# A hybrid decoder trunk on one core: gate weights loaded among the first values, more partners at the phase's front, a pair's copies in one turn, the last root ahead of the last products

## The chip, the cores and the metric

The kernel runs on one core of a Trainium2 chip. The time is the device time of one execution in microseconds (us); the median of the runs shown is what is compared. A profile is one more execution, recorded by the hardware profiler. Its engines are PE (TensorE, the matmuls; PEld is its loading of the stationary operand), DVE (VectorE), ACT (ScalarE), POOL (GpSimd) and SP (SyncE, which here only issues transfers). A name with a q behind it (SPq, POOLq) is the instruction queue of that engine. "L444" is line 444 of the kernel.

## The reference

One decoder layer over 256 tokens of width 2048, all in 32-bit floats:

```python
h = rmsnorm(x, pre_norm_g)
a_q, a_k, a_v, a_g, a_lr, b_q, b_k, b_v, b_g, m_a, m_b = split(h @ w_in)

gk  = log_sigmoid(a_lr @ gla_gk_w2 + gla_gk_b) / 16          # forget gate, rank 16
o_a = gla_chunked(a_q, a_k, a_v, gk)                         # 4 heads, gated linear attention
y_a = (rmsnorm(o_a, gla_norm_g) * silu(a_g)) @ w_branch_a

o_b = diff_attention(b_q, b_k, b_v, lam)                     # 16 heads, softmax1 - lam * softmax2
y_b = (rmsnorm(o_b, diff_norm_g) * (1 - lam_init) * silu(b_g)) @ w_branch_b

out = (sigmoid(m_a) * y_a + sigmoid(m_b) * y_b) @ w_out
x   = x + rmsnorm(out, post_norm_g)
```

The weights take 201 MB and are read once from memory; most of the work is the matmuls of 256 tokens with these weights.

## The kernel before

**Halves.** Every weight matrix is read in tiles of up to 1 MB ("raw", three buffers) and used in two halves. `seq` lists all halves in the order of their use. For each half, `emit_half` splits the 32-bit weights into two parts: ACT rounds to the matmul's format (L261, "hi"), DVE subtracts that from the original (L262, "lo"). TensorE then multiplies hi with both parts of the tokens and lo with the first part. The hi and lo buffers are three each, and `take` lets the splits be written three halves ahead of the matmuls (AHEAD = 3). So the split of a half can run once TensorE has done with the half three before it. The tile of a half is loaded by SP, two halves ahead in the list (`load`), once one of the three raw buffers is free.

**The order of each engine.** Instructions are written in program order, and a planner then fixes the order of each engine's queue ahead of time, by when it reckons that an instruction's inputs are there and by the program order among those that are ready. `tc.keep_in_program_order(i)` puts i behind the instruction that was written just before it on the same engine; `tc.issue_after(i)` puts the TensorE instructions of a block behind i. Once built, each engine works through its queue in order.

**Side tasks.** Work beside the large products is written as generators in the list `tasks`; each `pump` advances the first one or two of them by one step (a "turn"). A task that has yielded "go" is also advanced by `pump_eager`, which stands in the middle between two pumps.

**Stages.** In the order of the program:

1. `first_joint` multiplies the first values (v0, 16 halves of 832 columns). From kt = 11 on each half pumps `load_constants` once: constants, three loads of masks. Then come v2 and v3 (`token_major`, 8 halves each), with pumps of two tasks after each half: `late`, `forget_gate` and `sum_operands`.
2. `forget_gate` zeroes a tile (L515), loads w2 into four strips of it (L517, POOL), waits a turn, transposes the low-rank columns, splits w2 (L533 to L535), and multiplies (L544).
3. The phase (L779 to L788). Six sets of weight columns are multiplied with seven products in place of eight (PRODUCTS = 1, 3, 5, 6, 2, 7, 4), two tiles each, which makes 6 x 7 x 2 = 84 slots of two halves. A product needs sums of weight blocks. Blocks a and b are loaded by `link`, c by SP; further blocks are added to a and b in place by POOL's accumulating transfers (L198) and by DVE (L206). After product 1 has split a tile of a, the transfer that adds to it is issued; product 5 uses the result. Each slot is followed by one half of other work ("partner"): v4, k and q, the first two groups' dq and dk, and m00, 80 halves in all. Four slots, (s, 2, 0) for s = 1 to 4, have no partner, so that the counts agree. Within the phase every matmul is pinned to the program order.
4. Gated linear attention (`gla_scores`, `gla_out`), then differential attention in pairs of heads (`diff_pair`), beside the products of the gates and branches. A pair loads its q into kh and its k into kl (`twice`), copies kh to q2 (L960, ACT), subtracts into q2 from kh (L963, DVE), yields "go", copies kl over kh (L965, ACT) and subtracts (L966, DVE). The scores' matmuls (L982, L983) follow a pump later.
5. The output products for column groups 0 to 2 go over both token blocks; group 3 is kept split in memory and multiplied first for block 0 (512 columns), then for block 1 in two banks of 256 columns. Each bank's squares go to ACT with a running sum (L1150), its product with the norm's gain to DVE (L1154). The root of a block is a power on POOL (L352). The block is then scaled and added to x in four parts (L1170), each of which is stored by SP or ACT as `PARTS` says (L1171).

Of the kernel before, what the change touches and what calls it, by code (L numbers as in the profile page):

```python
# [8 lines left out]
BF16 = mybir.dt.bfloat16  # L9
U8 = mybir.dt.uint8  # L10
AF = mybir.ActivationFunctionType
ALU = mybir.AluOpType
AX = mybir.AxisListType

P = 128
D = 2048
# [6 lines left out]
RANK = 16  # L23
# [4 lines left out]
PRODUCTS = (1, 3, 5, 6, 2, 7, 4)  # L28
SETS = 6
# [5 lines left out]
PARTS = ((0, 768, 0), (1024, 1664, 1), (1664, 2048, 0), (768, 1024, 1))  # L35
# [40 lines left out]
def phase_steps():  # L76

    keys = ["v4"] + [f"{name}{hf}{c}" for hf in range(2) for name in ("k", "q") for c in range(4)]
    keys += [f"{name}{g}{c}" for g in EARLY for pair in range(2) for name in ("dq", "dk") for c in (2 * pair, 2 * pair + 1)]
    keys += ["m00"]  # L80
    other = [(key, r, h) for key in keys for r in range(4 if key in ("v4", "m00") else 1) for h in range(2)]
    slots = [(s, prod, t) for s in range(SETS) for prod in PRODUCTS for t in range(2)]
    skip = [(s, 2, 0) for s in range(1, SETS)][: len(slots) - len(other)]
    mixed = []
    for slot in slots:
        mixed += [("set", *slot, h) for h in range(2)]
        if slot not in skip:
            mixed.append(other.pop(0))
    return mixed + other

# [2 lines left out]
def hybrid_kernel(ctx: ExitStack, tc, xt, xn, preg, postg, w, w2, gkb, glag, lamv, diffg, ident_d, causal_d, lmask_d, out):  # L93
    nc = tc.nc
    pe, act, dve, pool, sp = nc.tensor, nc.scalar, nc.vector, nc.gpsimd, nc.sync
# [12 lines left out]
    def u(shape, name, dtype=F32):  # L108
        count[0] += 1
        return big.tile(shape, dtype, tag="u", name=f"{name}_{count[0]}")  # L110
# [5 lines left out]
    def sm(shape, name, dtype=F32, bufs=2):  # L116
        count[0] += 1
        return pools[0].tile(shape, dtype, tag=name, name=f"{name}_{count[0]}", bufs=bufs)
# [197 lines left out]
    diffg_s = const.tile([P, 1], F32, name="diffg_s")  # L316
    lam_s = sm([P, 4, 64], "lam_s", bufs=1)

    def load_constants():
        tc.keep_in_program_order(sp.dma_start(ident, ident_d))  # L320
        for t, src in ((gkb_s, gkb), (glag_s, glag), (diffg_s, diffg), (causal, causal_d)):
            tc.keep_in_program_order(sp.dma_start(t, src))
        tc.keep_in_program_order(sp.dma_start(lam_s, lamv.partition_broadcast(P)))
        yield
        for n in range(0, len(LEVELS) + 2, 4):
            m = min(4, len(LEVELS) + 2 - n)
            t = u([P, 4, S], "lmask")
            tc.keep_in_program_order(sp.dma_start(t[:, :m, :], lmask_d[:, n : n + m, :]))
            pool.tensor_copy(lmask[:, n : n + m, :], t[:, :m, :])
            yield  # L330

    ones = const.tile([P, P], F32, name="ones")
    dve.memset(ones, 1.0)
# [174 lines left out]
    def lend(tag, name, dtype=F32):  # L508

        count[0] += 1  # L510
        return blocks.tile([P, 8, P], dtype, tag=tag, name=f"{name}_{count[0]}", bufs=1).rearrange("p a t -> p (a t)")

    def forget_gate():
        w2_raw = lend("s2h", "w2_raw")
        tc.keep_in_program_order(dve.memset(w2_raw, 0.0))  # L515
        for i in range(4):
            pool.dma_start(w2_raw[32 * i : 32 * i + RANK, :], w2)  # L517
        yield
        yield
        bank = ps("bg")  # L520
        for b in range(2):
            pe.transpose(bank[:, P * b : P * b + P], lr[:, b, :], ident)
        top = t2([P, 512], "lrh").bitcast(F32R)
        lrt = sm([P, S], "lrt", F32R, bufs=1)
        act.activation(top[:, :S], bank[:, :S], AF.Copy)
        for i in (0, 64):
            act.activation(lrt[i : i + 32, :], bank[i : i + 32, :S], AF.Copy)
            r = slice(i + 32, i + 64)
            dve.tensor_tensor(out=lrt[r, :], in0=bank[r, :S], in1=f32(top[r, :S]), op=ALU.subtract)
        w2_s = lend("s2l", "w2_s", F32R)  # L530
        top = lend("r3h", "w2h", F32R)
        r = slice(64, P)
        act.activation(w2_s[:64, :], w2_raw[:64, :], AF.Copy)  # L533
        act.activation(top[r, :], w2_raw[r, :], AF.Copy)
        dve.tensor_tensor(out=w2_s[r, :], in0=w2_raw[r, :], in1=f32(top[r, :]), op=ALU.subtract)  # L535
        yield
        gp.extend(u([P, 2, 4, P], "gp") for _ in range(2))
        for hf in range(2):
            for c in range(2):
                bank = ps("bg")  # L540
                for i in range(2):
                    ct = 4 * hf + 2 * c + i
                    o = bank[:, S * i : S * i + S]
                    pe.matmul(o, w2_s[:, P * ct : P * ct + P], lrt, start=True, stop=True)  # L544
                for i in range(2):
                    ct = 4 * hf + 2 * c + i
                    act.activation(gp[hf][:, :, 2 * c + i, :], bank[:, S * i : S * i + S].rearrange("p (b t) -> p b t", b=2), AF.Identity, bias=gkb_s[:, ct : ct + 1])
            yield
        e = [lend(tag, "e") for tag in ("r3h", "r3l")]
        z = [t.rearrange("p b c t -> p (b c t)") for t in gp]  # L550
        for hf in range(2):
            act.activation(e[hf], z[hf], AF.Abs)
            yield
            act.activation(e[hf], e[hf], AF.Exp, scale=-1.0)
            yield
        for hf in range(2):
            act.activation(e[hf], e[hf], AF.Ln, bias=1.0)
        for hf in range(2):
            yield
            dve.scalar_tensor_tensor(out=z[hf], in0=z[hf], scalar=0.0, in1=e[hf], op0=ALU.min, op1=ALU.subtract)  # L560
        done.add("gate")
# [368 lines left out]
    for g in range(4):  # L930
        banks = token_major(f"ag{g}", 512, x_ops, 2)
        t = u2([P, 2, 512], "ua")
# [15 lines left out]
    def diff_pair(g, pair, values):  # L948
# [12 lines left out]
        for m in range(2):  # L961
            other = slice(64 - 64 * m, P - 64 * m)
            dve.tensor_tensor(out=q2[other, m], in0=f32(kh[other, m]), in1=f32(q2[other, m]), op=ALU.subtract)  # L963
        yield "go"
        tc.keep_in_program_order(act.activation(kh, f32(kl), AF.Copy))  # L965
        dve.tensor_tensor(out=kl, in0=f32(kl), in1=f32(kh), op=ALU.subtract)  # L966
        yield
# [69 lines left out]
        bank = ps("bg")  # L1037
# [4 lines left out]
        lo = ol[:, 2 * pair : 2 * pair + 2, :].rearrange("p h t -> p (h t)")  # L1042
# [78 lines left out]
    for g in range(4):  # L1121
        banks = token_major(f"y1{g}", 512, b_ops, 1 if g else 2, None if g else settle)
        for b in range(2):
            t = gb[g][:, b, :]
# [11 lines left out]
    for b in range(2):  # L1136
        xres.append([])
        for i in range(2):
            t = u([P, 1024], "xres")
# [3 lines left out]
    ssq = sm([P, 2, 5], "ossq", bufs=1)  # L1143
# [4 lines left out]
    def square(b, bank, n, i):  # L1148
        junk = sm([P, 512], "junk", BF16, bufs=1)
        act.activation(junk[:, :n], bank, AF.Square, accum_out=ssq[:, b, i : i + 1])  # L1150

    def gain(b, bank, lo, n):
        c = slice(lo % 1024, lo % 1024 + n)
        return dve.tensor_tensor(out=yg[b][lo // 1024][:, c], in0=bank, in1=pg[lo // 1024][:, c], op=ALU.mult)  # L1154

    def subtotal(b, parts):
        r = sm([P, 1], "or", bufs=2)
        dve.tensor_reduce(out=r, in_=ssq[:, b, :parts], op=ALU.add, axis=AX.X)
        dve.tensor_scalar(out=r, in0=r, scalar1=1.0 / D, scalar2=EPS, op0=ALU.mult, op1=ALU.add)
        return r  # L1160

    def last_part(b, bank, lo, n, i, r):
        square(b, bank, n, i)
        tc.keep_in_program_order(gain(b, bank, lo, n))
        tc.keep_in_program_order(dve.scalar_tensor_tensor(out=r, in0=ssq[:, b, i : i + 1], scalar=1.0 / D, in1=r, op0=ALU.mult, op1=ALU.add))
        rsqrt(r, r)
        for lo, up, queue in PARTS:
            c = slice(lo % 1024, lo % 1024 + up - lo)
            t, x = yg[b][lo // 1024][:, c], xres[b][lo // 1024][:, c]
            tc.keep_in_program_order(dve.scalar_tensor_tensor(out=t, in0=t, scalar=r, in1=x, op0=ALU.mult, op1=ALU.add))  # L1170
            (sp, act)[queue].dma_start(out[P * b : P * b + P, lo:up], t)  # L1171
# [6 lines left out]
    bank = ps("mm")  # L1178
    kept = []
    for q in range(8):  # L1180
        kept.append(take("o3"))
        for j in range(2):
            wh, wl = (t[:, 512 * j : 512 * j + 512] for t in kept[q])
            ah, al = (t[:, :P] for t in m_ops(2 * q + j))
            product(bank, ((ah, wh), (ah, wl), (al, wh)), q + j == 0, q == 7 and j == 1)
    last_part(0, bank, 1536, 512, 3, subtotal(0, 3))
    for c in range(2):
        bank = ps("mm")
        for kt in range(KT):
            lo = 512 * (kt % 2) + 256 * c  # L1190
            wh, wl = (t[:, lo : lo + 256] for t in kept[kt // 2])
            ah, al = (t[:, P:] for t in m_ops(kt))
            product(bank[:, :256], ((ah, wh), (ah, wl), (al, wh)), kt == 0, kt == KT - 1)
        if c == 0:
            square(1, bank[:, :256], 256, 3)
            gain(1, bank[:, :256], 1536, 256)
            r = subtotal(1, 4)
        else:
            last_part(1, bank[:, :256], 1792, 256, 4, r)


# [55 lines left out]
```

## Time and profile before

| what | us |
|---|---|
| median of three runs | 1126.66 (1126.32 to 1128.07) |
| the profiled execution's own time | 1126.1 |
| its span, first to last instruction | 1124.0 |
| TensorE busy | 1102.0 |
| VectorE busy | 850.5 |
| ScalarE busy | 673.6 |
| GpSimd busy | 111.2 |
| mean granted TensorE clock | 0.994 |

The span is what the profile's rows are measured against; the execution's own time is 2.1 us longer. A row of the timeline gives the start, the duration, the engine, the line, the operation and the tiles, out first, and in square brackets how long the engine was idle before it and what ended that. A row of the waits gives the total, the count and the longest. In the chain of waits, each piece is what the end of the span hung on at that time. A row for a stretch gives its length, the busy time of the five engines with their counts of instructions, the granted clock, the share of the transfer engines and GB/s.

### The profile page before, as it was taken

The page shows a single profiled execution, that of the slowest core. Times are in us where ns is not written, and L with a number is a line of the kernel's source. Part 1 is how long each engine was busy: PE and PEld are TensorE (multiplying, and loading weights), DVE is VectorE, ACT ScalarE, POOL GpSimd, SP SyncE. Part 2 cuts the span into 40 slices and gives each one's busy share as a digit, 9 for nine tenths or more (in the row PEclk, how much of TensorE's full clock was granted, in tenths as well). Part 3 has the DMA queues.
Part 4 walks back from the last instruction along what each step waited for, and adds up shares of the span by engine and source line. Part 5 has one row for each costly group of instructions (what it writes and reads, how often), then busy time and mean ns, then how long its engine had stood idle before and what let it go on. Part 6 is the DMA issues. An engine that isn't in the chain of part 4 may idle for free.

```text
span 1124.0 us, 15156 instructions
## 1 busy us (share of the span) xinstructions
PE 1102.0 (98%) x5546; PEld 943.2 (84%) x5546; DVE 850.5 (76%) x1185; ACT 673.6 (60%) x975; POOL 111.2 (10%) x172
## 2 busy tenths in 40 slices
PE   8999999999999999999999999999999999999996
PEld 7988788888888888888888888888888788888886
DVE  6787978879979789798898856959676854655463
ACT  6885666666666666666565555757575743444460
POOL 0202112021011210210200000010101010000000
PEclk9999999999999999999999999999999999999998
DMA  8879789699797987984844675958568675556752
GB/s 329 289 247 318 198 291 281 202 336 242 297 264 204 318 221 234 339 210 176 315 172 155 211 267 162 278 202 268 192 198 260 206 276 192 187 188 219 266 188 75
DMA packets 54042, 266.16 MB, mean 237 GB/s; under 512 B 6672, under 2 KB 8208, under 8 KB 34512
## 3 DMA queue, kind: packets, MB, share of 16 engines
q1 hardware_dynamic: 34848, 188.11, 48.5%
q0 software_dynamic: 18112, 75.77, 24.2%
q10 hardware_dynamic: 1008, 1.32, 0.4%
q8 instruction: 43, 0.70, 0.2%
q14 instruction: 31, 0.25, 0.1%
HBM read 244.20 MB, written 20.97 MB: 236 GB/s over the span
## 4 chain that ended last, share of the span: by engine, by line
PE 88%; DMA 3%; issue 3%; ACT 3%; DVE 2%; POOL 1%; DVEq 0%; SPq 0%; POOLq 0%; ACTq 0%
PE mm L444 60%; PE bg L444 18%; DMA a<-in_w_dram 2%; PE bg L432 2%; PE mm L432 2%; PE mm L417 2%; PE bg L860 1%; PE bg L417 1%; ACT hi L261 1%; PE bg L983 1%; DMA w_raw<-in_w_dram 1%; PE bg L982 1%; ACT prob L993 1%; ACT kh L965 0%; DMA raw<-in_w_dram 0%
## 5 line engine op out<-in xcount | busy, mean ns | idle before, releaser
L261 ACT ACTIVATE hi<-raw 128x1024 fp32r<-128x1024 f32 (+3 forms) x291 | 299.5, 1032 | 316.9 <-PE mm L444 207.5
L262 DVE TENSOR_TENSOR lo<-raw,hi 128x1024 fp32r<-128x1024 f32 (+3 forms) x291 | 345.2, 1189 | 176.1 <-ACT hi L261 173.3
L444 PE MATMUL mm<-hi,xs 128*128 128x512 f32 (+1 forms) x864 | 217.6, 387 | 0.2 <-ACT hi L261 0.2
L444 PEld LDWEIGHTS mm<-hi,xs 128*128 128x128 f32 x864 | 159.4, 188 | 26.7 <-ACT hi L261 0.7
L444 PE MATMUL bg<-xs,hi 128*128 128x512 f32 x512 | 131.9, 389 | 0.0
L262 DVE TENSOR_TENSOR lo<-a,hi 128x1024 fp32r<-128x1024 f32 x96 | 116.1, 1219 | 15.4 <-ACT hi L261 14.4
L261 ACT ACTIVATE hi<-a 128x1024 fp32r<-128x1024 f32 x96 | 101.6, 1061 | 34.1 <-PE mm L444 26.9
L444 PE MATMUL mm<-lo,xs 128*128 128x512 f32 (+1 forms) x432 | 119.4, 384 | 0.2 <-DVE lo L262 0.2
L444 PEld LDWEIGHTS bg<-xs,hi 128*128 128x128 f32 x512 | 96.2, 188 | 18.7
L444 PEld LDWEIGHTS mm<-lo,xs 128*128 128x128 f32 x432 | 80.9, 188 | 15.7 <-DVE lo L262 1.0
L444 PEld LDWEIGHTS bg<-xs,lo 128*128 128x128 f32 x512 | 69.8, 190 | 5.0
L444 PE MATMUL bg<-xs,lo 128*128 128x256 f32 x512 | 71.4, 282 | 0.0
L444 PE MATMUL mm<-xs,hi 128*128 128x512 f32 x256 | 67.3, 394 | 0.0
L262 DVE TENSOR_TENSOR lo<-b,hi 128x1024 fp32r<-128x1024 f32 x48 | 57.6, 1219 | 7.6 <-ACT hi L261 6.6
L261 ACT ACTIVATE hi<-b 128x1024 fp32r<-128x1024 f32 x48 | 50.8, 1060 | 13.9 <-PE mm L444 13.6
L444 PEld LDWEIGHTS mm<-xs,hi 128*128 128x128 f32 x256 | 46.1, 189 | 7.6
L444 PE MATMUL mm<-hi,oah 128*128 128x512 f32 x128 | 50.7, 396 | 0.0
L444 PE MATMUL mm<-hi,obh 128*128 128x512 f32 x128 | 50.4, 394 | 0.0
L444 PE MATMUL mm<-hi,oal 128*128 128x512 f32 x128 | 49.9, 390 | 0.0
L444 PE MATMUL mm<-hi,obl 128*128 128x512 f32 x128 | 49.9, 390 | 0.0
L993 ACT ACTIVATE prob<-prob,mx,score_scale 128x128 f32<-128x128 f32 x64 | 34.2, 537 | 10.9 <-DVE mx L988 10.9
L444 PE MATMUL mm<-hi,mh 128*128 128x512 f32 x96 | 37.5, 390 | 0.0
(284 smaller groups left out, 1874.2 us busy)
## 6 DMA issues: line engine op xcount, KB each, us to landing
raw<-in_w_dram SPq DMA_DIRECT2D x128, 1024.0 KB, 5.1
c<-in_w_dram SPq DMA_DIRECT2D x24, 512.0 KB, 10.5
a<-in_w_dram POOLq DMA_DIRECT2D x24, 512.0 KB, 12.2
b<-in_w_dram POOLq DMA_DIRECT2D x24, 512.0 KB, 8.9
raw<-in_w_dram SPq DMA_DIRECT2D x14, 832.0 KB, 7.1
a<-in_w_dram POOLq DMA_DIRECT2D x10, 1024.0 KB, 7.3
b<-in_w_dram POOLq DMA_DIRECT2D x10, 1024.0 KB, 7.5
kh<-dq SPq DMA_DIRECT2D x16, 256.0 KB, 8.3
```

The lines of the kernel that those rows point to most:

```text
L261: act.activation(hi_t[:, a:b], r[:, a:b], AF.Copy)
L262: dve.tensor_tensor(out=lo_t[:, a:b], in0=r[:, a:b], in1=f32(hi_t[:, a:b]), op=ALU.subtract)
L417: i = pe.matmul(out, lhs, rhs, start=first and n == 0, stop=last and n == len(pairs) - 1)
L432: i = pe.matmul(banks[g][b][:, :n], a[part][:, P * b : P * b + P], w[:, n * g : n * g + n], start=first, stop=last)
L444: i = pe.matmul(*args, **kw)
L860: pe.matmul(o, xk[:, P * c : P * c + P], xq.rearrange("p (b c t) -> p b c t", b=2, c=4)[:, :, c, :], start=i == 0, stop=i == 1)
L982: pe.matmul(banks[m][:, lo:up], q2[:, m, i2, t], kh[:, m, i2, :n], start=True, stop=False)
L983: pe.matmul(banks[m][:, lo:up], q2[:, m, i2, t], kl[:, m, i2, :n], start=False, stop=True)
L993: act.activation(prob[m][:, lo:up], prob[m][:, lo:up], AF.Exp, scale=score_scale[:, b : b + 1], bias=mx[:, i : i + 1], accum_out=z[:, i : ...
```

## The change

Four edits in one:

- `load_constants` gets a fifth turn, which zeroes the tile and loads w2 into it; `forget_gate` finds it there and has one turn less.
- In the first four slots of the phase, (0, 1, 0) to (0, 3, 1), two partner halves follow in place of one. In exchange (5, 2, 0) and (s, 4, 0) for s = 1 to 3 have none any more.
- `diff_pair` no longer yields "go" between its copies; both copies and all subtractions are written in one turn.
- `last_part` becomes `root` and `send`. The square of the last bank gets a tile of its own for its sum, the root is written ahead of that bank's gain, and block 0's last two parts are written behind block 1's first bank.

```diff
@@ -80,11 +80,13 @@
     keys += ["m00"]
     other = [(key, r, h) for key in keys for r in range(4 if key in ("v4", "m00") else 1) for h in range(2)]
     slots = [(s, prod, t) for s in range(SETS) for prod in PRODUCTS for t in range(2)]
-    skip = [(s, 2, 0) for s in range(1, SETS)][: len(slots) - len(other)]
+    front = [(0, prod, t) for prod in PRODUCTS[:2] for t in range(2)]
+    skip = [(s, 2, 0) for s in range(1, SETS)] + [(s, 4, 0) for s in range(1, SETS)]
+    skip = skip[: len(slots) + len(front) - len(other)]
     mixed = []
     for slot in slots:
         mixed += [("set", *slot, h) for h in range(2)]
-        if slot not in skip:
+        for _ in range((slot not in skip) + (slot in front)):
             mixed.append(other.pop(0))
     return mixed + other
 
@@ -316,6 +318,8 @@
     diffg_s = const.tile([P, 1], F32, name="diffg_s")
     lam_s = sm([P, 4, 64], "lam_s", bufs=1)
 
+    w2_tile = []
+
     def load_constants():
         tc.keep_in_program_order(sp.dma_start(ident, ident_d))
         for t, src in ((gkb_s, gkb), (glag_s, glag), (diffg_s, diffg), (causal, causal_d)):
@@ -328,6 +332,10 @@
             tc.keep_in_program_order(sp.dma_start(t[:, :m, :], lmask_d[:, n : n + m, :]))
             pool.tensor_copy(lmask[:, n : n + m, :], t[:, :m, :])
             yield
+        w2_tile.append(lend("s2h", "w2_raw"))
+        tc.keep_in_program_order(dve.memset(w2_tile[0], 0.0))
+        for i in range(4):
+            pool.dma_start(w2_tile[0][32 * i : 32 * i + RANK, :], w2)
 
     ones = const.tile([P, P], F32, name="ones")
     dve.memset(ones, 1.0)
@@ -511,11 +519,7 @@
         return blocks.tile([P, 8, P], dtype, tag=tag, name=f"{name}_{count[0]}", bufs=1).rearrange("p a t -> p (a t)")
 
     def forget_gate():
-        w2_raw = lend("s2h", "w2_raw")
-        tc.keep_in_program_order(dve.memset(w2_raw, 0.0))
-        for i in range(4):
-            pool.dma_start(w2_raw[32 * i : 32 * i + RANK, :], w2)
-        yield
+        w2_raw = w2_tile[0]
         yield
         bank = ps("bg")
         for b in range(2):
@@ -961,7 +965,6 @@
         for m in range(2):
             other = slice(64 - 64 * m, P - 64 * m)
             dve.tensor_tensor(out=q2[other, m], in0=f32(kh[other, m]), in1=f32(q2[other, m]), op=ALU.subtract)
-        yield "go"
         tc.keep_in_program_order(act.activation(kh, f32(kl), AF.Copy))
         dve.tensor_tensor(out=kl, in0=f32(kl), in1=f32(kh), op=ALU.subtract)
         yield
@@ -1159,12 +1162,15 @@
         dve.tensor_scalar(out=r, in0=r, scalar1=1.0 / D, scalar2=EPS, op0=ALU.mult, op1=ALU.add)
         return r
 
-    def last_part(b, bank, lo, n, i, r):
-        square(b, bank, n, i)
-        tc.keep_in_program_order(gain(b, bank, lo, n))
-        tc.keep_in_program_order(dve.scalar_tensor_tensor(out=r, in0=ssq[:, b, i : i + 1], scalar=1.0 / D, in1=r, op0=ALU.mult, op1=ALU.add))
+    def root(b, bank, n, r):
+        junk = sm([P, 512], "junk", BF16, bufs=1)
+        last = sm([P, 1], "olast", bufs=2)
+        act.activation(junk[:, :n], bank, AF.Square, accum_out=last)
+        tc.keep_in_program_order(dve.scalar_tensor_tensor(out=r, in0=last, scalar=1.0 / D, in1=r, op0=ALU.mult, op1=ALU.add))
         rsqrt(r, r)
-        for lo, up, queue in PARTS:
+
+    def send(b, r, parts):
+        for lo, up, queue in parts:
             c = slice(lo % 1024, lo % 1024 + up - lo)
             t, x = yg[b][lo // 1024][:, c], xres[b][lo // 1024][:, c]
             tc.keep_in_program_order(dve.scalar_tensor_tensor(out=t, in0=t, scalar=r, in1=x, op0=ALU.mult, op1=ALU.add))
@@ -1183,7 +1189,10 @@
             wh, wl = (t[:, 512 * j : 512 * j + 512] for t in kept[q])
             ah, al = (t[:, :P] for t in m_ops(2 * q + j))
             product(bank, ((ah, wh), (ah, wl), (al, wh)), q + j == 0, q == 7 and j == 1)
-    last_part(0, bank, 1536, 512, 3, subtotal(0, 3))
+    r0 = subtotal(0, 3)
+    root(0, bank, 512, r0)
+    tc.keep_in_program_order(gain(0, bank, 1536, 512))
+    send(0, r0, PARTS[:2])
     for c in range(2):
         bank = ps("mm")
         for kt in range(KT):
@@ -1193,10 +1202,13 @@
             product(bank[:, :256], ((ah, wh), (ah, wl), (al, wh)), kt == 0, kt == KT - 1)
         if c == 0:
             square(1, bank[:, :256], 256, 3)
-            gain(1, bank[:, :256], 1536, 256)
-            r = subtotal(1, 4)
+            tc.keep_in_program_order(gain(1, bank[:, :256], 1536, 256))
+            r1 = subtotal(1, 4)
+            send(0, r0, PARTS[2:])
         else:
-            last_part(1, bank[:, :256], 1792, 256, 4, r)
+            root(1, bank[:, :256], 256, r1)
+            tc.keep_in_program_order(gain(1, bank[:, :256], 1792, 256))
+            send(1, r1, PARTS)
 
 
 def kernel(**inputs):
```

## The prediction

> **What bounds the kernel now.** I read the page's busy times first, then TensorE's waits, then the stages in which those waits lie.
>
> ```profile
> PE 1102.0 (98%) x5546; PEld 943.2 (84%) x5546; DVE 850.5 (76%) x1185; ACT 673.6 (60%) x975; POOL 111.2 (10%) x172
> ```
>
> TensorE is busy for 1102.0 of the span's 1124.0 us, and the change leaves its matmuls as they are. So only 22 us can be fought over: the waits, the clock lost behind them, and the two ends. TensorE's waits by cause (us in total, times, longest):
>
> ```profile
> PE bg L982 <- ACT kh L965: 4.0, 4, 2.2
> PE mm L444 <- ACT hi L261: 2.2, 3, 1.7
> PE bg L544 <- DVE w_s L535: 2.0, 1, 2.0
> PE bg L983 <- DVE kl L966: 0.8, 3, 0.3
> ```
>
> Each of the four parts of the change meets one place: L444 the phase's front, L544 the gate weights, L982 and L983 the pairs; the fourth is the tail, where the matmuls are over. I take them by size.
>
> **The phase's front.** First TensorE's timeline: four places at which one tile of a set's product begins or resumes. Then the chain of waits (start, length). Then the stretches (granted clock third from last).
>
> ```profile
> 101.51 0.40 PE L444 MATMUL mm<-hi,s4h 128*128 128x512 f32 x1
> 106.46 0.40 PE L444 MATMUL mm<-hi,r1h 128*128 128x512 f32 x1
> ...
> 115.61 0.50 PE L444 MATMUL mm<-hi,r1h 128*128 128x512 f32 x1 [1.69 <-ACT hi L261]
> ...
> 121.18 0.39 PE L444 MATMUL mm<-hi,s2h 128*128 128x512 f32 x1
> ```
>
> ```profile
> 92.07 22.33 DMA a<-in_w_dram
> ...
> 129.05 2.18 PE bg L444 x12
> ```
>
> ```profile
> 116.00:118.00 2.00, 1.94 (x8) 1.37 (x7) 2.00 (x3) 2.00 (x3) 0.00 (x0) 0.87 1.01 205
> 118.00:120.00 2.00, 2.00 (x7) 1.98 (x7) 2.00 (x3) 0.70 (x2) 0.86 (x1) 0.50 0.51 78
> 120.00:122.00 2.00, 2.00 (x9) 1.86 (x9) 2.00 (x2) 0.87 (x1) 0.34 (x1) 0.78 0.71 221
> ...
> 160.00:500.00 340.00, 340.00 (x1719) 290.12 (x1718) 1.00 0.86 263
> ```
>
> One slot of the phase (two halves of a set and one partner half) takes 106.46 - 101.51 = 4.95 us. The tile that begins at 106.46 and the next should end at 106.46 + 2 x 4.95 = 116.36; the following product begins at 121.18. The front loses 4.82 us, more than the wait of 1.69 us, since the clock then falls to 0.87, 0.50 and 0.78. From 160 to 500 nothing is lost. What is late is the accumulating transfer issued at 92.07, which lands at 114.40.
>
> The change puts four more partner halves of v4, 2.18 us each, into the first four slots: these take 7.13 us instead of 4.95, beginning at 106.46 - 4 x 4.95 = 86.66. The half that waits is due at 106.46 + 4.95 + 1.39 (half of a set's 4.95 - 2.18 = 2.77) = 112.8 without a wait; now 8.72 us later, 121.5. Its transfer is issued behind the split of that tile's first pass, and that split comes at most the first slot's extra half, 2.18 us, later: landing at 114.40 to 116.6, split (about 1.1 us on ACT, 1.2 on DVE) by 118.9. The wait is covered with 2.6 us to spare.
>
> What is late next are the partners' own loads, on SP's queue (issue time; KB and us from issue to landing):
>
> ```profile
> 93.08 0.33 SPq L224 DMA_DIRECT2D raw<-in_w_dram  x1
> ...
> 102.91 25.52 SPq L224 DMA_DIRECT2D raw<-in_w_dram  x3
> ```
>
> ```profile
> raw<-in_w_dram SPq DMA_DIRECT2D x1, 800.0 KB, 15.4
> ```
>
> ```profile
> raw<-in_w_dram SPq DMA_DIRECT2D x1, 1024.0 KB, 14.4
> ```
>
> The first is v4's last tile, the second the first tile of k: they land at 108.5 and 117.3. With two halves a slot v4's last tile is due at 86.66 + 3 x 7.13 + 2.77 = 110.8, so its split must begin by about 109.7; it has 1.2 us, a little more because its buffer comes free earlier. The k tile is due at 86.66 + 4 x 7.13 + 2.77 = 117.95. Its buffer comes free some 5 us earlier (v4's second tile is used up in the second slot, no longer in the third and fourth), but it stands behind the same loads. If it still lands at 117.3, its split ends at 118.4: a wait of 0.4 us. **I take -4.7**, between 0 (a new wait of the old size) and -4.82.
>
> [...]
>
> The halves moved forward are missing later: one partner fewer in three slots (s,4,0) and one (s,2,0). Such gaps exist now at (s,2,0), here in the second set:
>
> ```profile
> 208.79 5.46 PE mm L444 x24
> 214.25 2.77 PE bg L444 x16
> ```
>
> 24 set matmuls run without a partner and the next group begins at 208.79 + 5.46 = 214.25: no wait. DVE's adds come in the slot behind (s,2,0) but not in (s,4,0) or the one behind it, so these are the easier places. Cost 0; if they had none of that cover, one split pair of 2.3 us each, 9 us in four places.
>
> **The gate weights.**
>
> ```profile
> 48.96 1.01 DVE L262 TENSOR_TENSOR lo<-raw,hi 128x832 fp32r<-128x832 f32 x1
> 50.13 0.91 DVE L515 MEMSET w_raw<- 128x1024 f32 x1 [0.16 <-DVE lo L262]
> ...
> 62.80 1.22 DVE L535 TENSOR_TENSOR w_s<-w_raw,w2h 64x1024 fp32r<-64x1024 f32 x1
> ```
>
> ```profile
> 51.33 1.93 POOL L517 DMA_DIRECT2D w_raw<-in_w_dram  x4 [2.46 <-DVE w_raw L515]
> ```
>
> ```profile
> 58.67 1.06 ACT L533 ACTIVATE w_s<-w_raw 64x1024 fp32r<-64x1024 f32 x1 [2.39 <-DMA w_raw<-in_w_dram]
> ```
>
> The memset, four transfers, landing, two ACT copies and a subtraction set when L544 runs. The memset is written one turn earlier, in the fifth turn of the constants' task (kt = 15). But it is pinned behind the DVE instruction written before it, and by then `take` has written the split of half 18, the third half of v2: the row at 48.96. So the memset can begin at 49.97 in place of 50.13: 0.16 us. POOL sat idle for 2.46 us before the four issues (0.48 us each), so passing its queue changes nothing, and nothing queues behind them. The gate's transposes and products are also written a turn earlier, but they wait for these weights. **I take -0.15**, between +0.5 (the products placed earlier among v2's while the weights are not) and -2.0 (the whole wait).
>
> **The pairs.**
>
> ```profile
> 714.77 1.40 DVE L963 TENSOR_TENSOR q<-kh,q 64x512 fp32r<-64x512 f32 x2
> ...
> 877.35 1.40 DVE L963 TENSOR_TENSOR q<-kh,q 64x512 fp32r<-64x512 f32 x2
> ```
>
> ```profile
> 716.26 1.06 ACT L965 ACTIVATE kh<-kl 128x1024 fp32r<-128x1024 f32 x1 [0.59 <-ACT dk L661]
> ...
> 878.83 1.06 ACT L965 ACTIVATE kh<-kl 128x1024 fp32r<-128x1024 f32 x1 [0.86 <-ACT hi L261]
> ```
>
> ```profile
> 879.94 0.44 PE L982 MATMUL bg<-kh,q 128*128 128x128 f32 x2 [2.21 <-ACT kh L965]
> ```
>
> Without "go" the second copy (L965) is written before the next half's split instead of behind it. But it overwrites kh, which the subtractions L963 read: they end at 716.17 and 878.75, and the copies begin 0.09 and 0.08 us later. The idle time put down to dk and hi is this wait. So the copy can't come earlier wherever it is written, and at these pairs TensorE waits as before. What may move is the subtraction L966, no longer behind a split of 1.2 us: up to the 0.8 us of the L983 waits. **I take -0.1**, between -4.8 (both rows of waits) and +13.7 (below).
>
> **The tail** (DVE, then TensorE, then ACT).
>
> ```profile
> 1110.93 0.69 DVE L1154 TENSOR_TENSOR yg<-mm,pg 128x512 f32<-128x512 f32 x1 [3.66 <-ACT junk L1150]
> ...
> 1112.38 2.74 DVE L1170 SCALAR_TENSOR_TENSOR yg<-yg,or,xres 128x768 f32<-128x768 f32 x4 [0.69 <-POOL or L352]
> 1115.04 0.41 DVE L1154 TENSOR_TENSOR yg<-mm,pg 128x256 f32<-128x256 f32 x1
> ...
> 1116.11 0.42 DVE L1154 TENSOR_TENSOR yg<-mm,pg 128x256 f32<-128x256 f32 x1 [0.41 <-ACT junk L1150]
> ...
> 1117.27 2.74 DVE L1170 SCALAR_TENSOR_TENSOR yg<-yg,or,xres 128x768 f32<-128x768 f32 x4 [0.67 <-POOL or L352]
> ```
>
> ```profile
> 1114.14 0.28 PE L417 MATMUL mm<-hi,ml 128*128 128x256 f32 x1
> ```
>
> ```profile
> 1114.23 1.27 ACTq L1171 DMA_DIRECT2D out_dram<-yg  x2
> 1115.60 0.38 ACT L1150 ACTIVATE junk<-mm 128x256 bf16<-128x256 f32 x1 [3.61 <-DVE or L1158]
> ```
>
> The last matmul ends at 1114.42, but the last square begins at 1115.60: it writes into the tile of sums that L1158 reads, and that stands behind block 0's four stores. From the end of the gain (1116.53) root update and POOL take 0.74 us to 1117.27.
> Afterwards: block 0's root starts at 1110.93 with its gain (0.69) under POOL's turn, so stores begin at about 1111.7. Two parts (1408 of 2048 columns of 2.74 us) end at 1113.6. The gain of block 1's first bank with its subtotal (0.66) ends at 1114.3, the other two parts (0.86) at 1115.15. The last square has a tile of its own, begins at about 1114.5, and takes 0.5. The root goes at 1115.2, the last stores at 1115.95 instead of 1117.27. **I take -1.3.** The other end is -0.4: if ACT issues block 0's last store ahead of that square, the square begins at 1115.6 as now, and only the 0.42 of the gain is saved.
>
> **Sum:** -4.7 - 0.15 - 0.1 - 1.3 = -6.25 us. The profiled execution took 1126.1 (2.1 of it outside the span), the median is 1126.66, 0.56 above. From the median: **1120.4**.
>
> **Rivals.** (1) The gate's wait goes after all: the 2.0 us of its row, 1118.5. For it: only 2 us are lacking. Against it: the pin.
> (2) The wait at the front is passed on to the partners' loads. Spare is 1.2 us. A last v4 tile 3 us later (its neighbour in the queue took 14.4 us for 1 MB, so such spreads occur) makes TensorE wait 1.8, and the clock falls again, 4.82 - 1.69 = 3.1: the front is worth nothing, 1126.66 - 1.55 = 1125.1. Against it: the buffer is free earlier than now. [...]
> (3) The pairs' waits vanish, 4.8 - 0.1 more: 1115.7. Against it: the copies' starts.
> (4) **Slower.** TensorE's order is fixed beforehand. If the copy, thought ready sooner, draws the scores forward to right behind a half at all eight pairs, each waits as at 879.94: 8 x 2.21 - 4.0 = +13.7, less 6.15 elsewhere: 1134.2. It decides once the mean wait passes (6.15 + 4.0) / 8 = 1.3 us a pair. Against it: three of the four waits share 1.8 us, and the copy is not ready sooner.
>
> **How the numbers follow.** Forecast 0.57, (1) 0.15, (2) 0.15, (3) 0.06, (4) 0.07. A measurement here tells about 0.2% (2.25 us) from no change. The forecast, (1), (3) and the mildest fifth of (2) are faster: 0.81; the rest of (2) no change: 0.12; (4) slower: 0.07. The range 1116.5 to 1125.2 goes from both smaller gains together to rival (2), and leaves out (3) and (4), 0.13.
>
> **What would show it.** Right: TensorE without a wait between 86 and 125, clock 1.00 there; L544 still waiting about 2 us with the memset near 50; L965 within 0.1 us of L963's end and its four waits left; the last square at the last matmul's end. Wrong: a wait on a partner's load near 109 or 117; L544 without a wait; scores waiting at more than four pairs; the last square behind ACT's store issue.

## The result, and the profile after

| | before | after |
|---|---|---|
| median of five executions each | 1127.76 us | 1120.01 us |
| lowest to highest | 1126.32 to 1131.18 | 1119.00 to 1123.41 |
| the profiled execution's own time | 1126.1 | 1123.41 |
| its span | 1124.0 | 1121.6 |

The ratio of after to before is 0.9938, with a 95% interval of 0.9911 to 0.9964: faster by 0.6%. Forecast were 1120.4 us, in a range of 1116.5 to 1125.2. The profiled execution of after is the longest of its five, so its rows show more loss than the median has; what that loss is, is worked out below.

The page's busy times and TensorE's waits of the changed kernel (us in total, times, longest):

```profile
PE 1101.9 (98%) x5546; PEld 944.8 (84%) x5546; DVE 851.3 (76%) x1185; ACT 673.9 (60%) x975; POOL 111.2 (10%) x172
```

```profile
PE bg L985 <- ACT kh L968: 4.2, 4, 2.5
PE bg L548 <- DVE w_s L539: 2.9, 1, 2.9
...
PE bg L986 <- DVE kl L969: 1.0, 4, 0.3
PE mm L452 <- ACT hi L263: 0.2, 1, 0.2
```

(L444 is now L452, L544 is L548, L965 is L968, L982 and L983 are L985 and L986; the kernels of the experiments move these lines by a few again.) The wait of the phase's products is gone. The gate's and the pairs' are still there, and a little longer than before.

**Front.** TensorE's timeline where product 5 begins, and the stretch that holds the phase's front:

```profile
117.41 0.40 PE L452 MATMUL mm<-hi,r1h 128*128 128x512 f32 x1
```

```profile
86.00:130.00 44.00, 44.00 (x224) 40.02 (x223) 34.09 (x36) 27.40 (x34) 9.04 (x12) 1.00 1.04 319
```

No idle time, clock 1.00. That gain can be read between two fixed points, the phase's first matmuls and the first gate (tanh) behind the phase. The first two rows are from before, the other two from after:

```profile
86.70 1.09 PE L444 MATMUL mm<-hi,xs 128*128 128x512 f32 x4
```

```profile
611.12 1.25 ACT L492 ACTIVATE tanh<-mm,half_rstd 128x512 f32<-128x512 f32 x2
```

```profile
88.92 1.09 PE L452 MATMUL mm<-hi,xs 128*128 128x512 f32 x4
```

```profile
608.00 1.25 ACT L500 ACTIVATE tanh<-mm,half_rstd 128x512 f32<-128x512 f32 x2
```

The way from the one to the other took 524.42 us and now takes 519.08: 5.3 us less. But the phase begins 2.2 us later. That is lost at the gate weights.

**Gate weights.** The memset, the transfers' issue, the first copy and the products, then the granted clock (third from last) in three stretches behind the wait:

```profile
50.06 0.91 DVE L336 MEMSET w_raw<- 128x1024 f32 x1 [0.16 <-DVE lo L264]
```

```profile
59.48 1.06 ACT L537 ACTIVATE w_s<-w_raw 64x1024 fp32r<-64x1024 f32 x1 [3.28 <-DMA w_raw<-in_w_dram]
```

```profile
64.99 1.15 PE L548 MATMUL bg<-lrt,w_s 128*128 128x256 f32 x8 [2.86 <-DVE w_s L539]
```

```profile
62.76:66.17 3.41, 1.18 (x10) 1.21 (x11) 3.35 (x5) 3.36 (x5) 0.00 (x0) 1.00 0.72 246
66.17:69.58 3.41, 3.41 (x11) 3.26 (x10) 3.41 (x5) 3.41 (x9) 0.00 (x0) 0.50 0.33 76
69.58:73.00 3.42, 3.42 (x19) 3.38 (x19) 2.26 (x4) 3.42 (x5) 0.00 (x0) 1.00 0.86 285
...
875.13:878.54 3.41, 1.17 (x6) 1.04 (x7) 3.38 (x6) 2.27 (x3) 0.00 (x0) 1.00 0.31 67
878.54:881.95 3.41, 3.41 (x13) 2.90 (x12) 3.34 (x17) 0.90 (x1) 0.00 (x0) 0.50 0.71 279
```

The memset begins behind the same split as before. The weights land later in this execution (median of the four transfers 7.7 us from issue to landing, 7.0 before), the wait is 2.86 us in place of 1.97, and the clock then falls to 0.50 for 3.41 us, which loses 1.7 us. The last two rows are the fourth pair: a wait of 2.5 us in place of 2.21, and 1.7 us of clock lost again, where before the clock stayed at 1.00.

**Pairs.** The end of the subtraction that reads kh, the copy over kh, and the scores that wait for it:

```profile
711.66 1.40 DVE L967 TENSOR_TENSOR q<-kh,q 64x512 fp32r<-64x512 f32 x2
```

```profile
713.14 1.06 ACT L968 ACTIVATE kh<-kl 128x1024 fp32r<-128x1024 f32 x1 [0.60 <-ACT dk L665]
```

```profile
714.25 0.44 PE L985 MATMUL bg<-kh,q 128*128 128x128 f32 x2 [0.59 <-ACT kh L968]
```

The copy begins 0.08 us behind the subtraction's end (713.06), as it did.

**Tail.** The last matmul, the last square, the last scaling:

```profile
1113.13 0.28 PE L425 MATMUL mm<-hi,ml 128*128 128x256 f32 x1
```

```profile
1113.51 0.38 ACT L1168 ACTIVATE junk<-mm 128x256 bf16<-128x256 f32 x1 [2.52 <-PE mm L425]
```

```profile
1114.84 2.74 DVE L1176 SCALAR_TENSOR_TENSOR yg<-yg,or,xres 128x768 f32<-128x768 f32 x4 [0.33 <-POOL or L360]
```

The square starts 0.10 us behind the last matmul's end (1113.41) and the scaling 1.43 us behind it. Before, these were 1.18 and 2.85 us: 1.42 us saved.

### The profile page after: what moved, and what is told of

It reads as the page before. It is cut to its first block, busy times and chain, and to the rows that moved or that the text cites. A ratio compares the mean times of both kernels' runs of the same rounds, so it can differ in the third digit from the quotient of the medians.

```text
span 1121.6 us, 15155 instructions
## 1 busy us (share of the span) xinstructions
PE 1101.9 (98%) x5546; PEld 944.8 (84%) x5546; DVE 851.3 (76%) x1185; ACT 673.9 (60%) x975; POOL 111.2 (10%) x172
## 5 line engine op out<-in xcount | busy, mean ns | idle before, releaser
L452 PE MATMUL mm<-hi,xs 128*128 128x512 f32 (+1 forms) x864 | 218.7, 388 | 0.2 <-ACT hi L263 0.2
L452 PEld LDWEIGHTS mm<-hi,xs 128*128 128x128 f32 x864 | 160.6, 189 | 26.9 <-ACT hi L263 0.5
L452 PE MATMUL bg<-xs,hi 128*128 128x512 f32 x512 | 131.9, 389 | 0.0
L452 PE MATMUL mm<-lo,xs 128*128 128x512 f32 (+1 forms) x432 | 119.6, 384 | 0.1
L452 PEld LDWEIGHTS bg<-xs,hi 128*128 128x128 f32 x512 | 96.3, 188 | 18.7
L452 PEld LDWEIGHTS mm<-lo,xs 128*128 128x128 f32 x432 | 81.4, 189 | 15.2 <-DVE lo L264 0.4
L452 PEld LDWEIGHTS bg<-xs,lo 128*128 128x128 f32 x512 | 69.8, 190 | 5.0
L452 PE MATMUL bg<-xs,lo 128*128 128x256 f32 x512 | 71.4, 282 | 0.0
L452 PE MATMUL mm<-xs,hi 128*128 128x512 f32 x256 | 67.3, 394 | 0.0
L452 PEld LDWEIGHTS mm<-xs,hi 128*128 128x128 f32 x256 | 46.1, 189 | 7.6
L452 PE MATMUL mm<-hi,oah 128*128 128x512 f32 x128 | 50.9, 398 | 0.0
L452 PE MATMUL mm<-hi,obh 128*128 128x512 f32 x128 | 50.4, 394 | 0.0
L452 PE MATMUL mm<-hi,oal 128*128 128x512 f32 x128 | 50.3, 393 | 0.0
L452 PE MATMUL mm<-hi,obl 128*128 128x512 f32 x128 | 49.9, 390 | 0.0
L452 PE MATMUL mm<-hi,mh 128*128 128x512 f32 x96 | 37.5, 390 | 0.0
```

Source lines behind the costliest of these rows:

```text
L452: i = pe.matmul(*args, **kw)
```

## The experiments

**Front and tail alone, and both together.** Each is the kernel before with that part's edit only. The front:

```diff
-    skip = [(s, 2, 0) for s in range(1, SETS)][: len(slots) - len(other)]
+    front = [(0, prod, t) for prod in PRODUCTS[:2] for t in range(2)]
+    skip = [(s, 2, 0) for s in range(1, SETS)] + [(s, 4, 0) for s in range(1, SETS)]
+    skip = skip[: len(slots) + len(front) - len(other)]
...
-        if slot not in skip:
+        for _ in range((slot not in skip) + (slot in front)):
```

> The kernel before with the phase's order alone changed (four more partner halves in the first four slots). Theory of the prediction: the wait of 1.69 us and the clock behind it go, -4.8 us (1.69 + 0.36 of waits, the rest clock), no wait of TensorE from 86 to 125 us and clock 1.00 there. Rival (the wait passed on to the partners' loads): a new wait near 109 or 117 us and 0 to -2 us. [...]

Measured: 0.9956 of before (0.9943 to 0.9970), which is 5.0 us less of 1126.47 (3.4 to 6.4). TensorE's waits:

```profile
PE bg L984 <- ACT kh L967: 3.6, 4, 1.8
PE bg L546 <- DVE w_s L537: 3.5, 1, 3.5
```

None is left in the phase, and the clock is 1.00 from 86 to 130. The gain is more than the waits alone, 1.69 + 0.36 us: behind them the clock had been at 0.50 for 3.41 us in before. The gate's wait is 3.5 us here, although this kernel's gate code is the old one: that wait varies by itself (1.2 to 3.5 us in the profiles of before and of the experiments that keep this code).

The tail, `last_part` replaced by `root` and `send` as in the change:

> The kernel before with the tail alone changed. Theory: the last square starts within 0.2 us of the last matmul's end, the last stores' instructions about 1.3 us earlier behind it: -1.3 us. Rival: ACT's store issue still stands ahead of the square: -0.4 us.

Measured: 0.9985 (0.9972 to 0.9998), 1.7 us less (0.2 to 3.2). In its timeline the last matmul ends at 1111.72, the square starts at 1111.81 and the last scaling 1.43 us behind the matmul: the theory, not the rival.

Both, with the gate weights and the pairs left as before:

> The changed kernel with the gate weights and the pairs as before. Theory (both parts do nothing): the same as the changed kernel within 0.3 us, 1126.7 - 6.1 = 1120 to 1121 us, L537's copy of the gate weights starting within 0.2 us of the changed kernel's place. Rival (the moved gate weights or the missing turn of the pairs cost what the changed kernel lost at its two waits, 0.9 us and 0.3 us and the clock behind them): 2 to 4 us faster than the changed kernel in every execution, with shorter waits than 2.86 and 2.5 us.

Measured: 1119.54 us, 0.9945 (0.9926 to 0.9964), beside 0.9938 (0.9911 to 0.9964) for the whole change. The two parts left out do nothing that can be measured. The rival falls: single executions of this kernel reach from 1117.95 to 1123.22, just like those of the whole change. So the times show no cost of the two parts. For the gate's wait the old code's own 1.2 to 3.5 us settle it. For the fourth pair's the rows leave more open: it took 1.8 to 2.3 us in the four profiles with the old code of the pairs, 2.4 to 3.5 in three with the new (leaving out the kernel with set waits around it). In the profiles of before and after that pair's second copy starts 2.85 and 2.86 us behind the start of the first, so between these two the difference lies in when ScalarE gets to the first copy, ahead of the edited place; whether the edit shifts that, the runs don't show.

**How many halves the front needs.** The changed kernel with one half more in the first slot only:

```diff
-    front = [(0, prod, t) for prod in PRODUCTS[:2] for t in range(2)]
+    front = [(0, 1, 0)]
```

> The changed kernel with one more partner half in the phase's first slot only, not in the first four. Theory (the late half is due 2.18 us later per added half, and its accumulating transfer is issued 2 us later because of the first added half): both move alike, a wait of 1.2 to 1.9 us stays in the second set product and the clock halves behind it: +3 to +5 us against the changed kernel. Rival (the landing is set by the shared transfers, not by the issue): the wait goes with one added half already, and the time is the changed kernel's.

Measured, in one execution: 1125.29 us, 5.3 above the changed kernel's median and just above what the theory had named. Yet the theory is wrong. The front has no wait:

```profile
PE bg L985 <- ACT kh L968: 5.2, 4, 3.5
PE bg L548 <- DVE w_s L539: 3.5, 1, 3.5
...
PE mm L452 <- ACT hi L263: 0.2, 1, 0.2
```

```profile
114.20 1.06 ACT L263 ACTIVATE hi<-a 128x1024 fp32r<-128x1024 f32 x1 [1.85 <-DMA a<-in_w_dram]
```

```profile
116.49 0.40 PE L452 MATMUL mm<-hi,r1h 128*128 128x512 f32 x1
```

The accumulating transfer was issued at 95.29 and had landed by 114.20, at most 18.9 us later; before it took 22.33 us. So its landing did not follow its issue, which was 3.22 us later than before's at 92.07. In this execution one half covers the wait; the time went to the gate (3.5 us) and the fourth pair (3.5 us), and to three stretches of halved clock behind them, 5.1 us. Why the fourth pair waited so long here is not shown. The time alone would nearly have confirmed the wrong story.

**Gate weights really early.** The changed kernel, with the memset and the loads in the first turn of the constants' task and the memset not pinned:

```diff
     def load_constants():
+        w2_tile.append(lend("s2h", "w2_raw"))
+        dve.memset(w2_tile[0], 0.0)
+        for i in range(4):
+            pool.dma_start(w2_tile[0][32 * i : 32 * i + RANK, :], w2)
         tc.keep_in_program_order(sp.dma_start(ident, ident_d))
...
-        w2_tile.append(lend("s2h", "w2_raw"))
-        tc.keep_in_program_order(dve.memset(w2_tile[0], 0.0))
-        for i in range(4):
-            pool.dma_start(w2_tile[0][32 * i : 32 * i + RANK, :], w2)
```

> The changed kernel with the memset and the four transfers of the gate weights in the first turn of the constants' task, the memset not pinned, so that they land before 50 us. Theory: the copy L537 then starts about 3.3 us earlier, near 56.2 us; the copies behind it follow, the subtraction ends near 61.6 us, before TensorE needs it at 62.1 us: the wait of L548 goes and the clock stays: -2 us against the changed kernel's faster executions and -4 to -5 us against its profiled one, about 1116 to 1118 us, with less spread. Rival: ScalarE's backlog, not the weights, is the limit: the wait shrinks by under 1 us and the time stays at 1119 to 1120 us.

Measured: 1117.48 us, 0.9918 (0.9901 to 0.9935). The memset now starts at the beginning of the kernel, and the gate's products come 9 us earlier and wait for nothing:

```profile
1.71 0.91 DVE L325 MEMSET w_raw<- 128x1024 f32 x1 [0.16 <-issue]
```

```profile
55.67 1.11 PE L548 MATMUL bg<-lrt,w_s 128*128 128x256 f32 x8
```

```profile
60.00:70.00 10.00, 10.00 (x55) 9.90 (x54) 8.68 (x12) 10.00 (x15) 1.07 (x2) 1.00 0.61 208
```

So the weights' arrival was the whole wait. The change's own edit does not bring it forward, since its memset still starts 0.16 us behind the split that it is pinned to. This run changed the turn and the pin at once, so it does not say whether an earlier turn with the pin would have been enough.

**The pair's copy in a tile of its own.**

```diff
+        kh = u([P, 2, 2, S], "kc", F32R)
         tc.keep_in_program_order(act.activation(kh, f32(kl), AF.Copy))
```

> The changed kernel with the pair's second copy written into a tile of its own, not over kh. Theory of the prediction (the copy is bound by the end of the subtractions that read kh): without that bond the copy follows the first one on ScalarE, 1.5 us or more ahead of the subtractions' end; the three waits of 0.58 us go, the fourth falls from 2.5 us to 1.5 us or less, and the clock behind it stays: -3 to -5 us against the changed kernel's profiled execution, -2 to -4 us against its median of 1120.0. Rival (ScalarE's own backlog binds the copy): the waits stay within 0.2 us and the time within 1 us.

Measured: 1119.39 us, 0.9931 (0.9915 to 0.9946): no gain over the changed kernel. Its profile has one more wait, of 1.73 us at 75.82, for a split among the values' halves, where no other profile shows more than 0.2 us, so the time alone does not size the edit. The copy does come earlier now, right behind the first. But the planner then puts the scores earlier too, and they wait for the subtractions (q, then kl). The fourth pair (L986 and L987 are the two products of the scores here):

```profile
870.60 0.30 PE L986 MATMUL bg<-kc,q 128*128 128x128 f32 x1 [0.84 <-DVE q L967]
871.22 0.33 PE L986 MATMUL bg<-kc,q 128*128 128x128 f32 x1 [0.33 <-DVE q L967]
...
872.36 0.44 PE L987 MATMUL bg<-kl,q 128*128 128x128 f32 x2 [0.53 <-DVE kl L970]
```

```profile
869.44:872.85 3.41, 1.72 (x10) 1.09 (x9) 3.35 (x5) 2.84 (x4) 0.00 (x0) 1.00 0.53 216
872.85:876.26 3.41, 3.41 (x11) 2.83 (x11) 3.41 (x16) 0.00 (x0) 0.00 (x0) 0.50 0.52 144
```

Neither theory nor rival: the waits are shorter, but here no wait over 0.84 us was needed to halve the clock. Three short ones close together (0.84, 0.33 and 0.53 us) did it. With the early gate weights as well:

> The changed kernel with the gate weights loaded in the first turn (as in the run before, 1117.5) and the pair's copy in a tile of its own. Theory: both gains add, 1113 to 1115 us, and the spread between executions falls under 2 us, since no wait of over 1.6 us is left behind the start. Rival (the spread has another source): executions still 3 us apart.

Measured: 1116.84 us, 0.9904 (0.9887 to 0.9922), executions 3.5 us apart. The rival's sign came: the scores wait 2.3 us on q, the fourth pair's clock still falls, and the spread stays. The gain over early weights alone is 0.6 us by the medians, within the noise.

**What halves the clock.** 22 waits of set length in the changed kernel's output stages:

```diff
+    def stall():
+        t = t2([P, 512], "stall")
+        pool.memset(t, 0.0)
+        bank = ps("bg")
+        tc.keep_in_program_order(pe.matmul(bank[:, :P], t[:, :P], t[:, :P], start=True, stop=True))
+        n = int(1050 * (d - 0.25))
+        while n > 0:
+            pool.memset(t[:, : min(n, 512)], 0.0)
+            n -= 512
+        tc.keep_in_program_order(pe.matmul(bank[:, :P], t[:, :P], t[:, :P], start=True, stop=True))
```

> The changed kernel with 22 set waits of TensorE between 920 and 1120 us, where it has none: each is a small matmul, GpSimd memsets of 1.2 to 3.6 us that wait for it, and a second matmul that waits for them (work that the reference does not have; nothing is left out). Theory (the clock halves for 3.4 us behind a wait by its length, with an edge near 2.2 us): waits under 2.0 us cost nothing beside themselves, all over 2.5 us lose 1.7 us of clock each; in between it varies. Rival (the clock is decided by the idle share of a window of fixed place): from about 1.7 us on some waits of each length lose the clock and some don't, the share rising with the length. [...]

The rival of a window of fixed place holds. Two of the waits, then stretches of 3.41 us laid where the clock's changes lie (length, then TensorE's busy time, clock third from last):

```profile
1127.39 0.49 PE L480 MATMUL bg<-stall 128*128 128x128 f32 x2 [1.80 <-POOL stall L478]
```

```profile
1033.57 0.49 PE L480 MATMUL bg<-stall 128*128 128x128 f32 x2 [2.81 <-POOL stall L478]
```

```profile
1124.62:1128.03 3.41, 1.61 (x10) 1.26 (x9) 1.23 (x1) 0.94 (x1) 1.57 (x3) 0.99 0.34 118
1128.03:1131.45 3.42, 3.42 (x10) 2.65 (x9) 0.00 (x0) 0.33 (x1) 0.00 (x0) 0.51 0.77 295
1029.05:1032.46 3.41, 1.71 (x9) 1.28 (x7) 1.44 (x2) 1.06 (x1) 1.52 (x3) 1.00 0.48 202
1032.46:1035.87 3.41, 2.30 (x11) 1.96 (x12) 0.00 (x0) 0.00 (x0) 0.94 (x3) 1.00 0.84 291
1035.87:1039.29 3.42, 3.42 (x19) 2.80 (x18) 1.82 (x2) 1.79 (x3) 0.00 (x0) 1.00 0.04 17
```

Behind the wait of 1.80 us, which lay in one such stretch, the clock was 0.51 in the whole next one. Behind the wait of 2.81 us, which a boundary cut into 1.70 and 1.11, it stayed at 1.00. From 850 to 1165 us the clock fell 14 times; read from stretches of half a microsecond, all the starts (940.26, 953.92, 970.99, 984.64, 1005.12, 1063.14 us and so on) lie a whole multiple of 3.413 us apart, to within 0.05 us (122.88 us, 36 steps, from the first to the last named). The waits' shares in each stretch of that grid, worked out from their starts and lengths, against the clock in the next:

| waits within one stretch of 3.41 us | stretches | next one at half clock |
|---|---|---|
| 1.99 us and more | 9 | 9 |
| 1.80 to 1.88 us | 4 | 3 |
| 1.56 to 1.70 us | 4 | 2 |
| up to 1.20 us, at full clock | 7 | 0 |
| 0.93 and 1.01 us, already at half clock | 2 | 2 |
| 0.08 and 0.20 us, already at half clock | 2 | 0 |

The shares are good to about 0.05 us. In the middle of the table the length of the waits does not decide alone. The profile of the copy's own tile has another stretch with TensorE busy for 1.72 us, the wait at 75.82, and there the clock stayed (first two rows; the fourth pair's are above). In the run with early gate weights as well, 1.35 us of waits were enough (last two rows):

```profile
74.13:77.54 3.41, 1.72 (x8) 1.42 (x8) 3.41 (x4) 3.41 (x5) 0.00 (x0) 1.00 0.91 305
77.54:80.96 3.42, 3.35 (x18) 3.26 (x18) 3.42 (x5) 2.26 (x3) 0.00 (x0) 1.00 0.45 141
...
867.33:870.74 3.41, 2.06 (x13) 1.39 (x11) 3.31 (x7) 3.41 (x4) 0.00 (x0) 1.00 0.69 281
870.74:874.15 3.41, 3.31 (x11) 2.93 (x12) 3.41 (x12) 0.02 (x1) 0.00 (x0) 0.50 0.35 77
```

At the pairs the matmuls between the waits are the scores' small ones. An estimate that counts this separates the cases better: give each matmul 0.23 us for every 512 columns, which is its step where nothing waits (the four from 136.60 on in before), and take the sum's share of the stretch. Over the profiles of all runs, from 14 us on to the last output products, each of the 24 stretches at full clock with a share under 0.34 was followed by a halved one, none with more than 0.42 was, and of the five between three were.

**One more turn ahead of the scores.** The kernel with early gate weights, and a second `yield` between the pair's copies and its scores, the copy over kh as before:

```diff
         dve.tensor_tensor(out=kl, in0=f32(kl), in1=f32(kh), op=ALU.subtract)
         yield
+        yield
         vv, uu = values
```

> The changed kernel with early gate weights and the same added turn, the second copy still over kh. Theory (the turn alone suffices, since the copy over kh ends 1.1 us behind the subtractions, well inside a turn of 2.7 us or more): 1111 to 1113 us, the four waits on kh gone. Rival (the copy must be free of kh): waits as in the run with early gate weights alone, 1117.5 us.

The same with the copy in a tile of its own as well:

> The kernel of the run with both gains (early gate weights, the pair's copy in its own tile) with one more turn between the pair's copies and its scores. Theory (in the own-tile run the scores were written forward to where the copies were thought ready, and waited there again, 0.7 to 0.8 us at each pair and in all 1.7 us in one stretch of 3.4 us at the fourth): one turn later the copies and subtractions are done, the 3.5 us of the pairs' waits go and the clock behind the fourth stays: 1111 to 1113 us. Rival (the scores are drawn forward again, or wait for something else a turn later): 1116 to 1117 us, as that run.

Measured: 1108.89 us, 0.9849 (0.9835 to 0.9863), and 1108.39 us, 0.9844 (0.9830 to 0.9858). That is 1.5% below before and 1% below the changed kernel, and both are 2 us or more under the 1111 to 1113 us expected. The own tile is not needed; it adds 0.5 us by the medians. All of TensorE's waits of the first one, and its stage of the pairs:

```profile
PE bg L346 <- DVE ones_b L343: 1.6, 1, 1.6
PE bg L440 <- ACT hi L263: 1.5, 1, 1.5
PE mm L440 <- ACT hi L263: 1.1, 2, 0.7
```

```profile
690.00:810.00 120.00, 120.00 (x692) 105.26 (x691) 89.44 (x217) 78.67 (x169) 10.92 (x17) 1.00 0.72 236
810.00:920.00 110.00, 110.00 (x562) 93.48 (x561) 82.88 (x201) 72.00 (x153) 9.86 (x16) 1.00 0.71 232
```

Nothing waits after the first values, and from 30 us on the clock is not halved once before the last matmul. The executions now lie within 0.46 and 0.53 us of each other. The gain over the kernel with early weights alone is 8.6 us by the medians and 9.2 by the spans (1116.0 to 1106.8): 4.9 us of waits, and TensorE's busy time is 4.9 us less (1099.3 to 1094.4), 1.7 of that from the clock and 1.3 at the scores' own rows; the waits among the first values are 0.9 us longer. Another 1.1 us of busy time lies at the seven matmuls ahead of the pairs' waits: such a row lasts 0.39 us, but where nothing waits the next matmul starts 0.23 us behind it (four took 1.09 us at 88.92 above), so each stop shows 0.16 us more. Where the last 0.8 us went the runs don't show. This busy time is why the gain passes the 6.6 us that waits and clock come to.

## Why the prediction was right

The forecast case came, with 1120.0 us for 1120.4. That the two lie so close is partly luck: before's median was 1126.66 when the forecast was worked out and is 1127.76 with two more executions, so 7.75 us came off by the medians (4.1 to 10.0 by the interval) where 6.25 were forecast. By its steps:

- **Front, -4.7.** Measured -5.0 alone (-3.4 to -6.4), and -5.3 between the two fixed points. The arithmetic of the slots held: the partners' loads, the next in line, made nothing wait. Of the half microsecond more than sized, some 0.3 us is one more stop before, too short for the table of waits: a product's matmul due at 137.52 (four from 136.60 on, 0.23 us apart) started at 137.75, and the next one at 138.32 in place of 138.20. The rest is not explained. One bound was a bound only: the half's transfer was given up to 2.18 us more because it is issued later, and the run with one half showed that its landing does not follow the issue. There one half was enough, so four may be more than the wait needs.
- **The clock in the front.** Taking 4.82 and not the 1.69 + 0.36 us of the waits alone was right, with some luck: a wait of this size did not always halve the clock. It did in both profiles that have it (before and the tail alone, 1.5 and 1.7 us of it in one stretch), but among the set waits only two of four stretches with 1.56 to 1.70 us did. The clock stayed halved for 3.41 us. Less idleness than such a stretch was enough: 1.80 to 1.88 us of 3.41 in three of four stretches among the set waits, and 1.35 at the fourth pair of the run with both gains. The grid of 3.413 us held through an execution (in after two halved stretches begin at 66.17 and 878.54, 238.0 grid steps apart), and it lay elsewhere in another (with the copy's own tile one begins at 872.85, 236.3 grid steps from 66.17).
- **Gate, -0.15.** Right in kind: the memset stayed behind the split that it is pinned to, and leaving this edit out changes nothing. The 0.15 us itself did not come, since the pause of 0.16 us behind the split stayed: the memset starts at 50.06 for 49.97 forecast. Rival (1), the wait gone, did not come; with the weights really early it does, and brings 2.5 us by the medians (1120.0 to 1117.5, with intervals that overlap) where the rival had 2.0.
- **Pairs, -0.1.** Right: the copy waits for the subtraction that reads kh, to 0.08 us. The 0.1 us hoped for at the second subtraction is not seen (1.0 us of waits in place of 0.8). Rival (4), scores drawn forward to wait, did not come in the change, but it is what the copy's own tile called up in a mild form.
- **Tail, -1.3.** Measured -1.42 in the profile, and -1.7 alone (-0.2 to -3.2). The square came ahead of ACT's store issue.

What the prediction lacked is the spread. It took the waits of 1.97 and 2.21 us that remain as worth what their rows say. In the profile of after each of the two waits cost 1.7 us of clock more, with 2.2 us of each in one stretch of the clock's grid. In the profile of before neither did; the fourth pair there:

```profile
875.25:878.66 3.41, 2.48 (x15) 1.86 (x13) 2.42 (x6) 2.72 (x6) 0.00 (x0) 1.00 1.01 420
878.66:882.08 3.42, 2.14 (x13) 1.88 (x14) 3.42 (x6) 2.01 (x2) 0.00 (x0) 1.00 0.36 81
882.08:885.49 3.41, 3.41 (x17) 2.84 (x17) 3.41 (x17) 2.93 (x8) 0.00 (x0) 1.00 0.60 245
```

A boundary cut the fourth pair's wait of 2.21 us into 0.93 and 1.28. In the profile of after, neither the gate's nor the fourth pair's was cut so (TensorE busy for 1.18 and 1.17 us of the two stretches), and that execution lost 2 x 1.7 us. This fits its 3.4 us above the median, and the mean clocks: 0.994 in the two executions of after at 1123.3 us, 0.996 to 0.998 in the other three. That those three escaped by the grid's place alone is inferred, since only one execution has a profile.

## What to carry to other kernels

A wait of TensorE cost its length here and, by chance, 1.7 us more: 1.35 us of waits within one stretch of 3.41 us were enough once, and none of the seven stretches with up to 1.20 us lost it among the set waits. So price a wait, or a group of short waits, of that size at its length plus up to 1.7 us, and let a profile of the kernel at hand decide. The spread between executions went from 3.5 us to 0.5 with the last of them here. Where a wait comes from work that is done too late for a fixed order, making that work earlier may only draw its user forward; letting the user come one turn later was worth 8.6 us here, where the earlier work was worth 0.6 at most. And read the rows behind a time that comes out as expected: one run had nearly the expected time for reasons that had nothing to do with it.

## What the runs showed of the hardware

In these runs the granted clock changed on a grid of 3.413 us. Among the set waits, each of the nine stretches in which TensorE idled for 1.99 us or more was followed by one at half clock, which lost 1.7 us, and none of the seven at full clock with 1.20 us or less was. In between, by the estimate above, it went more by how much the matmuls of the stretch worked than by the waits: 1.35 us among small matmuls (the fourth pair with both gains) were followed by 0.50, 1.69 us among large ones (at 74.13 with the copy's own tile) by 1.00. At half clock already, less idleness was enough: the fourth pair's 3.5 us in the run with one half in front reached 0.4 us into the halved stretch, and the clock was at 0.50 for 6.8 us in all.

The gate weights' four transfers, issued at 51.33 in before and at 51.26 in after, took 7.0 and 7.7 us (median) to land, and TensorE's wait was 1.97 and 2.86 us.
